# A hybrid DeltaNet and attention layer: diagonal blocks kept contiguous in DRAM and moved in few large DMAs, and the modulation's gate taken off TensorE

## The chip, the cores and the metric

The kernel runs on one core of a Trainium2 chip. The metric is the device time of one execution in microseconds (us). Three runs of the kernel before gave 2092.43, 2098.58 and 2100.68 us, so the median is 2098.58 us. The engines go by the profile's names: PE is TensorE (PEld its weight loads), DVE is VectorE, ACT is ScalarE, POOL is GpSimd and SP is SyncE, which issues most of the DMAs. An engine's name with a q (SPq) is its queue of DMA issues and waits.

## The reference

One layer of a diffusion backbone over 2048 latent tokens and 256 context tokens with a width of 1024, all in float32. What matters here, cut down:

```python
shift, scale, gate = jnp.split(jax.nn.silu(c) @ w_mod + b_mod, 3, axis=-1)
h = _rmsnorm(x, norm_w) * (1.0 + scale) + shift
# branch A: gated DeltaNet, 4 heads of 128, forwards and backwards, in chunks of 64:
a_mat = jnp.where(strict, jnp.einsum('nbhik,nbhjk->nbhij', kb, kc) * decay, 0.0)
t_mat = lax.linalg.triangular_solve(a_mat, eye, left_side=True, lower=True, unit_diagonal=True)
u = t_mat @ (vc * beta); w = t_mat @ (kb * exp(gc))         # and a scan over the chunks
# branch B: windowed attention with context keys and a sink; both branches gated:
y = sigmoid(ga) * (ya @ w_proj_a) + sigmoid(gb) * (yb @ w_proj_b)
x = x + gate[:, None] * (y @ w_out)
```

Two pieces of this are touched: the inverse of the unit lower triangular matrices of 64 by 64 (`t_mat`), one for each chunk of 64, head and direction, and the last third of the modulation, `gate`, a row of 1024 numbers that is needed only at the very end of the kernel.

## The kernel before

The kernel works through its stages in a fixed program: a Python function emits all instructions, and a scheduler with a timeline of its own sets the order on each engine when the program is built. Each engine then executes its list strictly in that order; SP's list holds the DMA issues. Matmuls of full accuracy are made of three (high part by high part, and two with a low part), so each weight tile is split into a high part on POOL (`wh`, L251) and a low part on DVE (`wl`, L252) after its DMA (`wr`, L250). A tile of weights for one group of 128 output channels is "a pair": two loads, two L251, two L252. Up to two pairs are held.

1. Up to about 118 us: modulation's shift and scale, the norms, and the normalised input `hh`, `hl`.
2. To about 630 us: the projections for q, k and v with short convolution (`qkv`, the tile `lps`), beside them the decays. For each key head and each 512 tokens `finish` multiplies keys by keys into `gps`, times the decays `dtl` (L607), and writes the result `p` and its transpose `pt` as full 128 by 128 blocks to DRAM (`Psp`, `PTsp`, L587): rows of 128 numbers, 512 bytes.
3. From about 620 to 963 us, the gates stage: `gates` (L814) runs 48 units of projections on PE (`rps`, L532 to L534, 24 matmuls a unit) for two of the four token groups. Beside them run two things. `mod_gate` computes the modulation's gate: it splits `w_mod` into high and low parts on POOL (`gwh` L227, `gwl` L228), multiplies them on PE (`gps` L230), adds two rows with a small matmul (`gsum` L236) and stores the row in `gsp`. And `base` inverts the triangular blocks on DVE: it fetches the two 64 by 64 diagonal blocks of each chunk of 128 and head, one block to a partition (`N`, L724, and the scale `nb`, L721), scales them (L725, L726), eliminates in 62 steps of two instructions (`btmp` L733, `N` L735), cuts the upper triangle off on POOL (L738), and writes the inverses to `Xsp` (L744). It does so twice, each time for 8 chunks and both directions; a third piece, `base4` (L748), does the last two chunks in another way.
4. From 963 to about 1385 us, the scan: 18 steps for both directions. `merge` builds the inverse for a chunk of 128 out of `Xsp` (`mx`, L966) and the off-diagonal block (`moff`, L968, read from `Psp` and `PTsp`); `chain` passes the state on; `output` writes results. More `rps` units fill the gaps on PE. Steps 1 to 8 need the first `base`, the next eight the second, the last two `base4`.
5. To the end: attention, projections of both branches, the output projection, where `gsp` is read.

The names in the program's order: `N`, `nb`, `btmp` are base's tiles; `x` (L1047, L1056), `S` (L1078) the scan's.

## Time and profile before

| what | value |
|---|---|
| runs | 2092.43, 2098.58, 2100.68 us; median 2098.58 us |
| the profiled execution's own time | 2097.5 us |
| its span, first to last instruction | 2095.8 us |
| PE busy | 1982.4 us, 95% |
| DVE, ACT, POOL busy | 1420.7, 751.5, 778.6 us |
| mean granted PE clock | 0.977 of full speed |
| DMA packets, bytes | 392748, 335.49 MB |

How to read the rows: a group's row names line, engine and operation, then what it writes and from what, the shape, the count, then its busy time and the mean of one instruction, and last how long the engine stood idle right before such instructions and what it waited for. A row of a table by stretches gives the stretch, its length, each engine's busy time with the number of instructions, the granted PE clock, the busy share of the DMA engines and GB/s. A row of the timeline gives start, duration and instruction, and in brackets the idle time before it. Matmuls are pipelined, so the modelled duration of one is longer than the distance between two starts, which is what counts.

### The profile page before, as it was taken

The numbers are of one execution on the slowest core, as the hardware profiler recorded it, in microseconds if no ns is written. First come the engines' busy times: TensorE is split into PE (matmuls) and PEld (weight loads), VectorE is DVE, ScalarE is ACT, GpSimd is POOL, SyncE is SP. The second block draws the span as 40 slices with busy tenths as digits, with TensorE's granted clock in tenths as the row PEclk, the third lists the DMA queues.
The fourth block names the chain that finished last, engine by engine and source line by source line (L and its number), as shares of the span: only waits on it lengthen the run. The fifth ranks groups of instructions, "written<-read, shape, count | busy, mean of one in ns | idle before, by whom it ended". The sixth has DMA issues, their size and how long they took to land.

```text
span 2095.8 us, 32306 instructions
## 1 busy us (share of the span) xinstructions
PE 1982.4 (95%) x11111; PEld 1650.2 (79%) x11111; DVE 1420.7 (68%) x2713; ACT 751.5 (36%) x1911; POOL 778.6 (37%) x920
## 2 busy tenths in 40 slices
PE   6999999999998789879988999999989999999999
PEld 3888888889986567667876888888878888878887
DVE  6888767767662799879945986644477777753322
ACT  5655555554441000001121223324466555541100
POOL 2862202255551356414232223422256454442321
PEclk8999999999999899999998999999999999999999
DMA  7452237754444533337567778855356555455542
GB/s 250 146 154 91 84 116 204 217 183 147 146 140 114 119 109 112 100 102 204 166 171 203 212 217 231 237 157 162 126 163 207 162 170 172 128 179 191 175 144 93
DMA packets 392748, 335.49 MB, mean 160 GB/s; under 512 B 83176, under 2 KB 318760, under 8 KB 392232
## 3 DMA queue, kind: packets, MB, share of 16 engines
q1 hardware_dynamic: 365160, 290.95, 48.0%
q10 hardware_dynamic: 27424, 42.48, 5.7%
q8 instruction: 88, 1.44, 0.3%
q14 instruction: 76, 0.62, 0.1%
HBM read 220.28 MB, written 111.49 MB: 158 GB/s over the span
## 4 chain that ended last, share of the span: by engine, by line
PE 67%; DVE 10%; DMA 9%; SPq 5%; POOL 4%; issue 3%; ACT 1%; POOLq 0%; DVEq 0%; ACTq 0%
PE rps L532 5%; PE rps L534 5%; PE rps L533 4%; PE lps L532 4%; PE lps L534 4%; PE lps L533 4%; PE ops L1270 3%; PE ops L1272 3%; PE ops L1271 3%; PE pt L920 3%; PE pps L1185 2%; PE pps L1187 2%; PE pps L1186 2%; DMA wr<-in_w_in_dram 2%; DVE btmp L733 2%
## 5 line engine op out<-in xcount | busy, mean ns | idle before, releaser
L532 PE MATMUL rps<-hh,wh 128*128 128x512 f32 x768 | 313.7, 408 | 6.9 <-DVE rt L798 5.6
L534 PE MATMUL rps<-hh,wl 128*128 128x512 f32 x768 | 312.1, 407 | 0.0
L533 PE MATMUL rps<-hl,wh 128*128 128x512 f32 x768 | 311.8, 406 | 0.0
L251 POOL TENSOR_SCALAR wh<-wr 128x512 fp32r<-128x512 f32 x120 | 105.5, 889 | 276.4 <-DMA wr<-in_w_in_dram 121.3
L796 ACT ACTIVATE rt<-rps 128x512 f32<-128x512 f32 x96 | 57.5, 599 | 387.5 <-PE rps L534 319.7
L532 PEld LDWEIGHTS rps<-hh,wh 128*128 128x128 f32 x768 | 147.9, 193 | 41.5 <-DVE rt L798 6.0
L534 PEld LDWEIGHTS rps<-hh,wl 128*128 128x128 f32 x768 | 147.9, 193 | 35.9 <-issue 2.2
L533 PEld LDWEIGHTS rps<-hl,wh 128*128 128x128 f32 x768 | 147.7, 192 | 32.5 <-issue 1.3
L532 PE MATMUL lps<-hh,wh 128*128 128x512 f32 (+1 forms) x448 | 171.9, 384 | 0.3 <-ACT y L632 0.3
L534 PE MATMUL lps<-hh,wl 128*128 128x512 f32 (+1 forms) x448 | 171.3, 382 | 0.0
L533 PE MATMUL lps<-hl,wh 128*128 128x512 f32 (+1 forms) x448 | 171.2, 382 | 0.0
L571 DVE SCALAR_TENSOR_TENSOR cacc<-y,cw,cacc 128x512 f32<-128x512 f32 (+1 forms) x224 | 160.4, 739 | 14.6 <-ACT cacc L569 11.8
L252 DVE TENSOR_TENSOR wl<-wr,wh 128x512 fp32r<-128x512 f32 x120 | 96.9, 818 | 66.6 <-POOL wh L251 64.4
L896 DVE CUSTOM_DVE_ANT_0 pr<-sc,band,sk 128x640 f32<-128x640 f32 (+1 forms) x128 | 106.7, 862 | 51.4 <-PE pt L920 25.9
L922 ACT CAST ph<-pt 128x512 fp32r<-128x512 f32 x156 | 90.4, 586 | 123.0 <-PE pt L920 92.5
L924 DVE TENSOR_TENSOR pl<-pt,ph 128x512 fp32r<-128x512 f32 x156 | 105.1, 685 | 37.1 <-ACT ph L922 36.4
L735 DVE TENSOR_TENSOR N<-N,btmp 128x62 f32<-128x62 f32 (+30 forms) x124 | 121.2, 978 | 2.7
L733 DVE TENSOR_TENSOR btmp<-N 128x62 f32<-128x62 f32 (+30 forms) x124 | 120.4, 971 | 3.0
L906 POOL TENSOR_SCALAR pr<-pr,sm 128x640 f32<-128x640 f32 (+1 forms) x128 | 99.8, 801 | 48.5 <-DVE sm L904 27.3
L898 ACT ACTIVATE pr<-pr,sm 128x640 f32<-128x640 f32 (+1 forms) x128 | 104.0, 815 | 20.2 <-DVE sm L896 19.9
L1185 PE MATMUL pps<-yh,wph 128*128 128x512 f32 x256 | 105.3, 415 | 3.9 <-ACT yh L1167 2.5
L1186 PE MATMUL pps<-yl,wph 128*128 128x512 f32 x256 | 101.6, 397 | 0.0
(307 smaller groups left out, 4974.6 us busy)
## 6 DMA issues: line engine op xcount, KB each, us to landing
wr<-in_w_in_dram SPq DMA_DIRECT2D x120, 256.0 KB
kw<-Ksp SPq DMA_DIRECT2D x28, 384.0 KB
x<-vsp SPq DMA_DIRECT2D x36, 256.0 KB
k<-ksp SPq DMA_DIRECT2D x34, 256.0 KB
kT<-kTsp SPq DMA_DIRECT2D x34, 256.0 KB
wm<-in_w_mod_dram SPq DMA_DIRECT2D x16, 512.0 KB
xt<-in_x_dram SPq DMA_DIRECT2D x16, 512.0 KB
dtl<-Dsp SPq DMA_DIRECT2D x32, 256.0 KB
```

The lines of the kernel that those rows point to most:

```text
L251: G.tensor_scalar(wh[:, k:k + 4], wr, 1.0, 1.0, op0=ALU.mult, op1=ALU.mult)
L532: T.matmul(ps, lhsT=wh[:, k], rhs=xh[:, k], start=k == 0, stop=False)
L533: T.matmul(ps, lhsT=wh[:, k], rhs=xl[:, k], start=False, stop=False)
L534: T.matmul(ps, lhsT=wl[:, k], rhs=xh[:, k], start=False, stop=k == kt - 1)
L571: V.scalar_tensor_tensor(a, y[:, t:t + n], cw[:, m, t:t + 1], a, op0=ALU.mult, op1=ALU.add)
L733: V.tensor_tensor(tv, A[:, m + 1:, m].unsqueeze(2).to_broadcast([h1 + n, r, m]), A[:, m, 0:m].unsqueeze(1).to_broadcast([h1 + n, r, m]), o ...
L735: V.tensor_tensor(A[:, m + 1:, 0:m], A[:, m + 1:, 0:m], tv, op=ALU.add)
L896: V.tensor_tensor_reduce(s_, ps[:, o:768], band[:, b0:b0 + W + 256], -0.125, sk[:, 1, hd:hd + 1], ALU.add, ALU.min, sm[:, h, 1:2])
L898: S.activation(s_, s_, AF.Exp, scale=-1.0, bias=sm[:, h, 1:2], accum_out=sm[:, h, 2:3])
L924: V.tensor_tensor(pl, pt, f32(ph), op=ALU.subtract)
L1185: T.matmul(ps, lhsT=wh[:, k, ms], rhs=hs[k], start=k == 0, stop=False)
L1186: T.matmul(ps, lhsT=wh[:, k, ms], rhs=ls[k], start=False, stop=False)
```

## The change

Three things are changed.

First, the DRAM layout. In place of `Psp` and `PTsp` there are `Nsp` (the two 64 by 64 diagonal blocks of a chunk and head, each contiguous) and `offsp` (the one off-diagonal block that `merge` reads), both for each direction. `finish` writes three pieces (`spill_blocks`) where it wrote one block. `base` then fetches runs of neighbouring chunks with one DMA each, and writes its inverses with one DMA for each direction to `Xset`; of each of these 8 chunks `merge` reads its part. `base4` fetches two chunks at once.

Second, in `base` the scaling on DVE and the select on POOL go over four pieces of 16 rows, and only over the columns that matter, where they went over the whole 64 by 64.

Third, `mod_gate` no longer uses PE for the product: ACT multiplies a tile of `w_mod` of 128 by 512 by the activated input (a number for each partition), POOL adds eight of these into `gacc`, and one matmul with a column of ones sums over the partitions; this happens twice, for 512 columns each.

```diff
@@ -94,11 +94,13 @@
     ksp = dscr("ksp", [NC, 128, H, 128])
     vsp = dscr("vsp", [NC, 128, H, 128])
     Dsp = dscr("Dsp", [NC, 128, H, 128])
-    Psp = dscr("Psp", [NC, 128, H, 128])
-    PTsp = dscr("PTsp", [NC, 128, H, 128])
+
+    Nsp = [dscr(f"Nsp{d}", [NC, H, 2, 64, 64]) for d in range(2)]
+    offsp = [dscr(f"offsp{d}", [NC, 64, H, 64]) for d in range(2)]
     QDsp = dscr("QDsp", [NB, 128, H, 128])
     brT = dscr("brT", [NC, 8, 128])
-    Xsp = [many(f"Xsp{d}_", NC, [H, 2, 64, 64]) for d in range(2)]
+    Xset = [many(f"Xsp{d}_", 2, [8, H, 2, 64, 64]) for d in range(2)]
+    Xsp = [{}, {}]
     X4sp = dscr("X4sp", [2, 2, 4, 8, 64, 16])
@@ -209,37 +211,26 @@
 
     def mod_gate(pool, ones):
 
-        for _ in range(3):
+
+        for n in range(2):
+            cs_ = slice(2 * D + n * 512, 2 * D + n * 512 + 512)
+            gacc = pool.tile([128, 512], F32, name="gacc", bufs=1)
+            for k in range(KT):
+                wm = pool.tile([128, 512], F32, name="wmg", bufs=2)
+                dma(wm, ins["w_mod"][0, k * 128:(k + 1) * 128, cs_])
+                S.activation(wm if k else gacc, wm, AF.Copy, scale=silc[:, k, 0:1])
+                if k:
+                    G.tensor_tensor(gacc, gacc, wm, op=ALU.add)
+                yield
             yield
-        sil2 = pool.tile([128, KT, 2], F32R, name="sil2", bufs=1)
-        V.tensor_copy(sil2[:, :, 0], silc[:, :, 0])
-        V.tensor_tensor(sil2[:, :, 1], silc[:, :, 0], f32(sil2[:, :, 0]), op=ALU.subtract)
-        for n in range(4):
-            gps = psum(f"gd{n % 2}", [2, 256], name=f"gps{n}")
-            ns = slice(n * 256, n * 256 + 256)
-            cs_ = slice(2 * D + n * 256, 2 * D + n * 256 + 256)
-            for k in range(0, KT, 2):
-                wm = wq.tile([128, 2, 256], F32, name="wmg", tag="wr")
-                dma(wm, ins["w_mod"][0, k * 128:(k + 2) * 128, cs_].rearrange("(k p) c -> p k c", p=128))
-                for j in range(2):
-                    wh = pool.tile([128, 256], F32R, name="gwh", bufs=1)
-                    wl = pool.tile([128, 256], F32R, name="gwl", bufs=1)
-                    G.tensor_scalar(wh, wm[:, j], 1.0, 1.0, op0=ALU.mult, op1=ALU.mult)
-                    G.tensor_tensor(wl, wm[:, j], f32(wh), op=ALU.subtract)
-                    for x in (wh, wl):
-                        T.matmul(gps, lhsT=sil2[:, k + j], rhs=x, start=k + j == 0 and x is wh,
-                                 stop=k + j == KT - 1 and x is wl)
-                yield
-            two = ev.tile([2, 256], F32, name="gtwo", tag="rt")
-            V.tensor_copy(two, gps)
-            gsum = psum(f"gd{n % 2}", [1, 256], name=f"gsum{n}")
-            T.matmul(gsum, lhsT=ones[0:2, 0:1], rhs=two, start=True, stop=True)
-            grow = ev.tile([1, 256], F32, name="grow", tag="rt")
+            gsum = psum(f"gd{n}", [1, 512], name=f"gsum{n}")
+            T.matmul(gsum, lhsT=ones[:, 0:1], rhs=gacc, start=True, stop=True)
+            grow = ev.tile([1, 512], F32, name="grow", tag="rt")
             dma(grow, ins["b_mod"][:, cs_])
             V.tensor_tensor(grow, gsum, grow, op=ALU.add)
             V.tensor_scalar(grow, grow, 0.5, None, op0=ALU.mult)
-            dma(gsp[:, ns], grow)
-        yield
+            dma(gsp[:, n * 512:n * 512 + 512], grow)
+            yield
 
@@ -578,6 +569,13 @@
         dma(dt, Dsp[c0:c0 + nn, :, h].rearrange("c p i -> p c i"))
         return dt
 
+    def spill_blocks(d, t, c0, nn, h):
+
+        for b in range(2):
+            r = slice(b * 64, b * 64 + 64)
+            dma(Nsp[d][c0:c0 + nn, h, b].rearrange("c r i -> r c i"), t[r, :, r])
+        dma(offsp[d][c0:c0 + nn, :, h].rearrange("c r i -> r c i"), t[64:128, :, 0:64])
+
...
@@ -605,7 +603,10 @@
                 T.matmul(gps[:, j], lhsT=zc[j] if m >= 4 else kT[:, j], rhs=zc[j], start=True, stop=True)
             p = pb.tile([128, 4, 128], F32, name="p", tag="o")[:, :nn]
             V.tensor_tensor(p, gps[:, :nn], dt, op=ALU.mult)
-            spill((Psp[c0:c0 + nn] if m >= 4 else QDsp[b0:b0 + nn])[:, :, h], p)
+            if m >= 4:
+                spill_blocks(1, p, c0, nn, h)
+            else:
+                spill(QDsp[b0:b0 + nn][:, :, h], p)
...
-            spill(PTsp[c0:c0 + nn, :, h], pt)
+            spill_blocks(0, pt, c0, nn, h)
 
@@ -705,7 +706,17 @@
     bs = bs_.__enter__()
 
 
-    def base(npool, pool, fr, bk):
+    def runs(chunks):
+
+        out = []
+        for i, c in enumerate(chunks):
+            if out and c == out[-1][1] + out[-1][2]:
+                out[-1][2] += 1
+            else:
+                out.append([i, c, 1])
+        return out
+
+    def base(si, npool, pool, fr, bk):
 
 
         n = 8 * len(fr)
@@ -716,14 +727,16 @@
             G.memset(N[0:h1], 0.0)
             G.memset(nb[0:h1], 0.0)
         for d, chunks in ((0, fr), (1, bk)):
-            for ci, c in enumerate(chunks):
-                p0 = d * h1 + ci * 8
-                dma(nb[p0:p0 + 8], brT[c, d * 4:d * 4 + 4].rearrange("h (b t) -> (h b) t", b=2))
-                for b in range(2):
-                    src = (PTsp, Psp)[d][c][b * 64:b * 64 + 64, :, b * 64:b * 64 + 64]
-                    dma(N[p0 + b:p0 + 8:2], src.rearrange("r h i -> h r i"))
-        V.tensor_tensor(N[0:h1], N[0:h1], nb[0:h1].unsqueeze(1).to_broadcast([h1, 64, 64]), op=ALU.mult)
-        V.tensor_tensor(N[h1:h1 + n], N[h1:h1 + n], nb[h1:h1 + n].unsqueeze(2).to_broadcast([n, 64, 64]), op=ALU.mult)
+            for i0, c, k in runs(chunks):
+                p0 = d * h1 + i0 * 8
+                dma(nb[p0:p0 + 8 * k], brT[c:c + k, d * 4:d * 4 + 4].rearrange("c h (b t) -> c (h b) t", b=2))
+                dma(N[p0:p0 + 8 * k], Nsp[d][c:c + k].rearrange("c h b r i -> (c h b) r i"))
+        for q in range(4):
+            r, w = slice(q * 16, q * 16 + 16), q * 16 + 16
+            V.tensor_tensor(N[0:h1, r, 0:w], N[0:h1, r, 0:w],
+                            nb[0:h1, 0:w].unsqueeze(1).to_broadcast([h1, 16, w]), op=ALU.mult)
+            V.tensor_tensor(N[h1:h1 + n, r, 0:w], N[h1:h1 + n, r, 0:w],
+                            nb[h1:h1 + n, r].unsqueeze(2).to_broadcast([n, 16, w]), op=ALU.mult)
         yield 9
         A = N[0:h1 + n]
         for m in range(1, 63):
@@ -735,13 +748,16 @@
-        G.affine_select(A, A, pattern=[[1, 64], [-1, 64]], base=0, channel_multiplier=0,
-                        compare_op=ALU.is_gt, fill=0.0)
+        for q in range(4):
+            r, w = slice(q * 16, q * 16 + 16), 64 - q * 16
+            G.affine_select(A[:, r, q * 16:], A[:, r, q * 16:], pattern=[[1, 16], [-1, w]], base=0,
+                            channel_multiplier=0, compare_op=ALU.is_gt, fill=0.0)
         V.memset(A.rearrange("p r c -> p (r c)")[:, ::65], 1.0)
         for d, chunks in ((0, fr), (1, bk)):
+            p0 = d * h1
+            dma(Xset[d][si].rearrange("c h b r j -> (c h b) (r j)"), N[p0:p0 + n].rearrange("p r j -> p (r j)"))
             for ci, c in enumerate(chunks):
-                p0 = d * h1 + ci * 8
-                dma(Xsp[d][c].rearrange("h b r c -> (h b) r c"), N[p0:p0 + 8])
+                Xsp[d][c] = Xset[d][si][ci]
         yield 1
 
     def base4(fr, bk):
@@ -755,12 +771,9 @@
         G.memset(nb[0:32], 1.0)
         G.memset(nc_, 1.0)
         for d, chunks in ((0, fr), (1, bk)):
-            for ci, c in enumerate(chunks):
-                p0 = d * 16 + ci * 8
-                dma((nc_, nb)[d][p0:p0 + 8], brT[c, d * 4:d * 4 + 4].rearrange("h (b t) -> (h b) t", b=2))
-                for b in range(2):
-                    src = (PTsp, Psp)[d][c][b * 64:b * 64 + 64, :, b * 64:b * 64 + 64]
-                    dma(N[p0 + b:p0 + 8:2], src.rearrange("r h i -> h r i"))
+            c, p0 = chunks[0], d * 16
+            dma((nc_, nb)[d][p0:p0 + 16], brT[c:c + 2, d * 4:d * 4 + 4].rearrange("c h (b t) -> c (h b) t", b=2))
+            dma(N[p0:p0 + 16], Nsp[d][c:c + 2].rearrange("c h b r i -> (c h b) r i"))
...
-    for fr, bk, np_ in (([0, 1] + LAT(*range(0, 6)), [0, 1] + LAT(*range(10, 16)), bs),
-                        (LAT(*range(6, 14)), LAT(*range(2, 10)), bs2)):
+    for si, (fr, bk, np_) in enumerate((([0, 1] + LAT(*range(0, 6)), [0, 1] + LAT(*range(10, 16)), bs),
+                                        (LAT(*range(6, 14)), LAT(*range(2, 10)), bs2))):
-            for _ in base(np_, bs2, fr, bk):
+            for _ in base(si, np_, bs2, fr, bk):
...
                 dma(X[b * 64:b * 64 + 64, :, b * 64:b * 64 + 64], Xsp[d][c][:, b].rearrange("h r c -> r h c"))
         off = pool.tile([128, H, 64], F32, name=f"moff{d}", bufs=2)
-        dma(off[64:128], (PTsp, Psp)[d][c][64:128, :, 0:64])
+        dma(off[64:128], offsp[d][c])
```

The order on the engines, from the built programs. PE in the gates stage; `rps` are the gates' own matmuls, `gps` the modulation's. Before, from the eighth unit of the stage on, it reads:

```order
L534 MATMUL rps<-hh_441,wl 128x512
L532 MATMUL rps<-hh_441,wh 128x512
L533 MATMUL rps<-hl_442,wh 128x512
L230 MATMUL gps_7833<-gwh,sil_7830 2x256
L534 MATMUL rps<-hh_441,wl 128x512
L532 MATMUL rps<-hh_441,wh 128x512
L230 MATMUL gps_7833<-gwl,sil_7830 2x256
L533 MATMUL rps<-hl_442,wh 128x512
```

and so on, 64 `gps` and 4 `gsum` in all (the trace counts each `gsum` twice, for two passes). After it, the only matmuls of the modulation in this stage are two `gsum`, the first of which stands 19 units into the stage:

```order
L523 MATMUL rps<-hh_155,wh 128x512
L524 MATMUL rps<-hl_156,wh 128x512
L525 MATMUL rps<-hh_155,wl 128x512
L227 MATMUL gsum_8317<-gacc,mats 1x512
L523 MATMUL rps<-hh_411,wh 128x512
L524 MATMUL rps<-hl_412,wh 128x512
```

In both programs the first matmul of the scan stands behind the same number of units, 49.7 counted from the stage's first.

SP's list at the start of the stage, where `base` is fed. Before:

```order
L721 DMA nb<-brT 8x64
L724 DMA N<-PTsp 4x64x64
L799 DMA zasp_149<-rt 128x512
L724 DMA N<-PTsp 4x64x64
L587 DMA QDsp<-p 128x4x128
L721 DMA nb<-brT 8x64
L724 DMA N<-PTsp 4x64x64 x2
L721 DMA nb<-brT 8x64
```

After:

```order
L732 DMA nb<-brT 64x1x64
L733 DMA N<-Nsp_89 64x4096
L812 DMA zasp_119<-rt 128x512
L585 DMA QDsp<-p 128x4x128
L732 DMA nb<-brT 16x1x64
L733 DMA N<-Nsp_90 16x4096
L732 DMA nb<-brT 48x1x64
L733 DMA N<-Nsp_90 48x4096
L241 DMA wr<-in_w_in_dram 128x4x128
```

For the two calls of `base`, 96 issues (32 `nb`, 64 `N`) became 10 (5 and 5).

DVE at the same place; L252 and L243 are the same line of `weights`, L798 and L811 the same of `rest_run`. Before:

```order
L252 TENSOR_TENSOR wl<-wr,wh 128x512
L725 TENSOR_TENSOR N<-N,nb 64x4096
L798 SCALAR_TENSOR_TENSOR rt<-rt,rps 128x512
L252 TENSOR_TENSOR wl<-wr,wh 128x512
L798 SCALAR_TENSOR_TENSOR rt<-rt,rps 128x512
L252 TENSOR_TENSOR wl<-wr,wh 128x512
L798 SCALAR_TENSOR_TENSOR rt<-rt,rps 128x512
L252 TENSOR_TENSOR wl<-wr,wh 128x512
L726 TENSOR_TENSOR N<-N,nb 64x4096
```

After:

```order
L736 TENSOR_TENSOR N<-N,nb 64x16x16
L736 TENSOR_TENSOR N<-N,nb 64x16x32
L736 TENSOR_TENSOR N<-N,nb 64x16x48
L736 TENSOR_TENSOR N<-N,nb 64x1024
L243 TENSOR_TENSOR wl<-wr,wh 128x512
L811 SCALAR_TENSOR_TENSOR rt<-rt,rps 128x512
L243 TENSOR_TENSOR wl<-wr,wh 128x512
L738 TENSOR_TENSOR N<-N,nb 64x16x16
L738 TENSOR_TENSOR N<-N,nb 64x16x32
L738 TENSOR_TENSOR N<-N,nb 64x16x48
L738 TENSOR_TENSOR N<-N,nb 64x1024
```

The scaling stands about two pairs of weights earlier, and the first elimination follows three pairs earlier. From there the steps lie closer: ahead of the scan's first L1056 stand 233 of the 248 elimination instructions, where 212 stood before. POOL's list has 14 additions to `gacc` in place of 64 instructions for `gwh` and `gwl`, and its eight selects stand between the `wh` of the pairs, each behind the elimination step that it waits for.

## The prediction

> **What bounds the kernel now.** I read the page first, then the busy times by stretches, then PE's and DVE's groups in the stretch that stood out.
>
> ```profile
> span 2095.8 us, 32306 instructions
> PE 1982.4 (95%) x11111; PEld 1650.2 (79%) x11111; DVE 1420.7 (68%) x2713; ACT 751.5 (36%) x1911; POOL 778.6 (37%) x920
> ```
>
> PE bounds the whole: 2095.8 - 1982.4 = 113 us are idle. The question is where they lie. Busy times by stretches (the first is the gates stage, the second the scan's start, the last the key projections):
>
> ```profile
> core 0: us, PE busy (x) PEld busy (x) DVE busy (x) ACT busy (x) POOL busy (x), PEclk, DMA share, GB/s
> 640.00:963.00 323.00, 278.94 (x1170) 211.53 (x1169) 250.44 (x273) 27.57 (x46) 118.58 (x117) 0.95 0.41 109
> 963.00:1100.00 137.00, 128.93 (x876) 110.02 (x875) 104.67 (x190) 26.51 (x70) 43.62 (x53) 0.94 0.69 188
> ...
> 310.00:424.00 114.00, 112.36 (x692) 97.99 (x691) 83.37 (x162) 67.03 (x222) 29.49 (x30) 1.00 0.74 211
> ```
>
> The gates stage alone has 323 - 278.94 = 44 us of PE's idle time. PE's groups in it:
>
> ```profile
> L533 PE MATMUL rps<-hl,wh 128*128 128x512 f32 x366 | 148.5, 406 | 0.0
> L532 PE MATMUL rps<-hh,wh 128*128 128x512 f32 x366 | 148.3, 405 | 5.6 <-DVE rt L798 5.6
> ...
> L230 PE MATMUL gps<-gwh,sil 128*2 128x256 f32 x32 | 9.2, 289 | 23.1 <-POOL gwh L227 23.1
> L230 PE MATMUL gps<-gwl,sil 128*2 128x256 f32 x32 | 9.2, 288 | 5.7 <-POOL gwl L228 5.6
> L236 PE MATMUL gsum<-gtwo,mats 2*1 2x256 f32 x8 | 2.8, 430 | 9.7 <-DVE gtwo L234 9.7
> ```
>
> Nearly all of it stands before the modulation's own matmuls: 23.1 + 5.7 + 9.7 = 38.5 us; the other 5.6 us is a wait for `rt` on DVE. PE never waits for a weight pair here. What a matmul really costs, from the timeline:
>
> ```profile
> 656.03 0.39 PE L534 MATMUL rps<-hh,wl 128*128 128x512 f32 x1
> ...
> 657.43 0.40 PE L534 MATMUL rps<-hh,wl 128*128 128x512 f32 x1
> ...
> 663.38 0.79 PE L532 MATMUL rps<-hh,wh 128*128 128x512 f32 x1 [5.56 <-DVE rt L798]
> ...
> 668.67 0.47 PE L532 MATMUL rps<-hh,wh 128*128 128x512 f32 x1
> ...
> 670.80 0.28 PE L230 MATMUL gps<-gwl,sil 128*2 128x256 f32 x1
> 670.92 0.40 PE L533 MATMUL rps<-hl,wh 128*128 128x512 f32 x1
> ...
> 907.09 1.01 PE L236 MATMUL gsum<-gtwo,mats 2*1 2x256 f32 x2 [9.71 <-DVE gtwo L234]
> ```
>
> Six matmuls lie between the first two rows: 1.40 / 6 = 0.233 us each. Twelve lie between the next two: 5.29 / 12 = 0.44 us, so a wait of 5.6 us is followed by matmuls at about half rate, and costs 12 x 0.21 = 2.5 us more. A `gps` takes 670.92 - 670.80 = 0.12 us.
>
> **The gates stage without its waits.** It holds 3 x 366 = 1098 `rps`: 1098 x 0.233 = 256 us of the 323. The rest, 67 us, is made of 44.1 us of waits, 64 x 0.12 = 7.7 us of `gps`, 4 x 1.0 = 4 us of `gsum`, and by difference 11 us of half-rate matmuls, about four waits' worth at 2.5 us. The order rows show that after the change no `gps` is left and the scan begins behind the same 49.7 units. So 38.5 + 7.7 + 11 us go. Of `gsum` I keep 2 us: two matmuls of twice the columns, instead of four. That the two don't wait: in POOL's order the last addition into each `gacc` stands some five weight pairs, or ten units of 24 x 0.233 = 5.6 us, ahead of the first `gsum` and eight pairs ahead of the second.
>
> The 5.6 us wait for `rt`, and base's start (DVE's groups in the stage, two rows of SP's issues with their durations and first and last start, a row of the timeline, one of the chain of waits):
>
> ```profile
> L725 DVE TENSOR_TENSOR N<-N,nb 64x4096 f32<-64x4096 f32 x2 | 8.8, 4417 | 18.8 <-DMA nb<-brT 18.8
> L726 DVE TENSOR_TENSOR N<-N,nb 64x4096 f32<-64x4096 f32 x2 | 8.8, 4422 | 11.4 <-DMA nb<-brT 9.1 <-issue 2.3
> L721 SPq DMA_DIRECT2D nb<-brT x32: 310/1086/2167, 624.0 to 728.7; - x32
> L724 SPq DMA_DIRECT2D N<-PTsp x32: 593/627/1376, 624.6 to 704.9; - x32
> ...
> 688.99 0.75 DVE L733 TENSOR_TENSOR btmp<-N 128x62 f32<-128x62 f32 x1
> 1140.14 9.34 DMA N<-N
> ```
>
> SP issued base's loads from 624.0 to 728.7 us; DVE stood 18.8 + 11.4 us for them, `rt` queued behind. Now there are ten issues. How long a load of 64 rows of 16 KB takes isn't shown; the nearest row is the copy of `N` (three of 512 KB in 9.34 us, 6.2 us a megabyte), and below it stands nothing but the DMA share in this stretch, 0.41, which says there is room. I take 6 us a megabyte: the first load lands near 632, the second near 638 us, and the first elimination can start near 644 instead of 688.99 us. The 5.6 us go, and I put back 3 us since DVE meets these waits earlier in its list, with `rt` and a weight pair behind them. Sum for the stage: -5.6 - 38.5 - 7.7 - 2 - 11 + 3 = **-62 us**.
>
> **DVE must keep up.** PE's stage shrinks to some 260 us, and the same eliminations have to fit beside it (groups in the stage of DVE and POOL, then of the whole span the nearest rows for an addition on POOL and a scaled copy on ACT, and the scan's first `ksps` in the chain of waits):
>
> ```profile
> L735 DVE TENSOR_TENSOR N<-N,btmp 128x62 f32<-128x62 f32 (+30 forms) x97 | 97.0, 1000 | 2.4
> L733 DVE TENSOR_TENSOR btmp<-N 128x62 f32<-128x62 f32 (+30 forms) x97 | 94.4, 973 | 2.5
> L252 DVE TENSOR_TENSOR wl<-wr,wh 128x512 fp32r<-128x512 f32 x46 | 35.1, 773 | 36.6 <-POOL wh L251 36.6
> L228 POOL TENSOR_TENSOR gwl<-wmg,gwh 128x256 fp32r<-128x256 f32 x32 | 37.8, 1182 | 2.5 <-PE gps L230 0.2
> L227 POOL TENSOR_SCALAR gwh<-wmg 128x256 fp32r<-128x256 f32 x32 | 23.6, 738 | 52.0 <-DMA wmg<-in_w_mod_dram 45.9 <-PE rps L532 3.4 <-PE gps L230 1.0
> L1153 POOL TENSOR_TENSOR wpl<-wpr,wph 128x512 fp32r<-128x512 f32 x16 | 20.4, 1296 | 10.7 <-ACT wph L1152 10.7
> L569 ACT ACTIVATE cacc<-y,cw 128x512 f32<-128x512 f32 (+1 forms) x56 | 38.3, 693 | 2.5 <-DMA cw<-in_conv_w_dram 1.3 <-DVE g L186 0.8
> 997.90 1.53 PE ksps L1054 x12
> ```
>
> Between base's start and the scan's first L1056 stand 233 elimination instructions at (97.0 + 94.4) / 194 = 0.99 us, 230 us; 25 weight pairs at 2 x 0.77, 39 us; and some 25 us of `rt`, the second base's scaling and the scan's first work. That is 294 us from 644, so 938 us. PE reaches the scan at 640 + 256 + 2 + 3 = 901 us, and from there the first `ksps` was 997.90 - 963 = 35 us away: 936 us. The two meet within 2 us, so DVE is no longer cover but a second bound. Against a delay: POOL's 37.8 + 23.6 = 61.4 us for the gate become 14 additions of 128 by 512, at 1.3 us (nearest row, L1153) 18 us, and the scaling shrinks by piece to 2560 of 4096 columns, 4 x (4.42 - 2.76) = 6.6 us in all, already counted. For a delay: nothing evens out inside single pairs. I charge **+5 us**; the ends are 0 and, if the eliminations run a tenth slower, +29. ACT's 16 products at 0.69 us (L569, also a scaled copy) are 11 us on an engine busy 27.57 of 323, behind which the `tanh` waits; I cost them at nothing, and return to it below. The select, split likewise, comes off POOL's list piece by piece and hides behind the `wh`, which wait for loads anyway.
>
> **The scan.** Two of PE's waits hang on what the change moves:
>
> ```profile
> PE mtp L974 <- POOL x L1047: 6.5, 1, 6.5
> PE mtp L974 <- DMA mx<-Xsp: 6.2, 1, 6.2
> L744 SPq DMA_DIRECT2D Xsp<-N x32: 285/651/2372, 872.8 to 1096.3; - x32
> ```
>
> The second base's 16 writes reach to 1096.3 us, in one list with the scan's own loads, up to 2.4 us an issue. They become two, and in DVE's new order base ends behind the first step that has an `x`, where it ended behind the third. Step 9 then finds its inverses, and the loads of `x` aren't queued behind writes. Both waits and their half-rate time go: -12.7 - 2 x 2.5 = **-18 us**. The bound on the other side is 0, if the scan waits elsewhere.
>
> **The key projections pay.**
>
> ```profile
> DVE p L607 <- DMA dtl<-Dsp: 6.2, 5, 2.1
> L587 SPq DMA_DIRECT2D Psp<-p x20: 359/360/611, 301.9 to 423.6; - x20
> ```
>
> Each of 40 writes becomes three: 80 more issues at 0.36 us, 29 us more on SP in about 114, with `dtl` and the weights behind them, some 1 us later each time. Rows: 36 full-size writes (16 full and 4 half, twice) of 512 rows of 512 bytes become 768 rows of 256. In this stretch the DMA engines were busy 0.74 x 16 x 114 = 1350 us for 24.1 MB, 47 thousand rows of 512 bytes, 29 ns each. If a half row costs half, DMA time falls, and PE, busy 112.36 of 114, gains nothing. If it costs the same, 9200 more rows add 265 us, and the share goes to 0.89. The trace shows no DRAM write of 256-byte rows; I take the same price, since the reads of 256-byte rows for `N` left the share at 0.41 beside the weights. PE then waits for `p` a little more often than the 6.2 us that DVE waits now: **+6 us**, between 0 and the rival below.
>
> [...]
>
> **Sum.** -62 + 5 - 18 + 6 = -69 us on the profiled run's 2097.5 us: 2028.5. That run lies 1.1 us under the median, so it makes no difference; I round to **2030 us**. Later stages have the same instructions; I expect nothing from them.
>
> **Rivals.**
> A. *DVE takes over.* The eliminations run at 0.99 us or worse and PE waits for weight pairs. For it: DVE is busy 250.44 of 323 now. Against: POOL disturbs less. Its upper price, 29 us in place of 5: about 2053. Chance 0.17.
> B. *The gate's new chain is the new wait.* ACT executes in order, its `tanh` frees PE's accumulators, and a product waits for a 256 KB load just when base's megabytes are fetched. For it: POOL waited 45.9 us for these loads. Against: two units of slack, and the first `gsum` ten units behind. Were half of the 38.5 us lost again: about 2050. Chance 0.10.
> C. *Half rows cost double* (57 ns). The writes take 27.6 thousand x 57 ns = 1580 us instead of 530: the share becomes 1.31, the stretch 36 us longer, 30 above my charge: 2060. Chance 0.10.
> D. *The weights bound the stage.* POOL's `wh` is ready late anyway, and PE's waits move to the pairs. Against: PE waits for no pair in the groups above. Half of the 62 us stays: about 2060. Chance 0.05.
> E. *Slower.* The same place as C, at a price that eats all: 69 us + 6 in a stretch of 114 means a share of 1.66, 3030 us of DMA, 80 ns a row. From 80 ns, 2.8 times the measured row, the kernel is slower; at 100 ns the stretch grows by another 34 us, 2130. Chance 0.04.
>
> **How the numbers follow.** The forecast has 0.54: between 2005 (no DVE charge, no charge in the projections, and a third wait of the scan gone) and 2045. The range reaches over A to D to **2005 to 2068**. About 0.5% (10 us) can be told from no change. Only E is slower; a mixture of C, A and D near zero has 0.03. Faster 0.93, same 0.03, slower 0.04.
>
> **What would show it.** Right: PE's groups in the gates stage without idle time, the scan's first matmul near 900 us, the first elimination near 645, DVE close to full until some 940, no wait for `mx`. Wrong: PE waiting for `wl` (A) or `rt` behind ACT (B); DMA share near 1 and waits for `dtl` between 310 and 430 us (C, E).

## The result, and the profile after

The change takes **2047.58 us** (median of four runs, 2046.15 to 2049.45) where the kernel before takes 2097.22 (2092.43 to 2100.68): a ratio of 0.9763, with a 95% interval from 0.9748 to 0.9778. The prediction was 2030 us, between 2005 and 2068. The gain is 50 us and not 68, and the time lies 2.6 us above the narrower interval, 2005 to 2045, to which the forecast itself gave a chance of 0.54.

The page of the profiled run, and its busy times by the stretches that the prediction used:

```profile
span 2044.3 us, 32068 instructions
PE 1966.8 (96%) x11043; PEld 1643.2 (80%) x11043; DVE 1421.5 (70%) x2715; ACT 760.4 (37%) x1927; POOL 742.9 (36%) x876
```

```profile
core 0: us, PE busy (x) PEld busy (x) DVE busy (x) ACT busy (x) POOL busy (x), PEclk, DMA share, GB/s
640.00:963.00 323.00, 312.39 (x1377) 247.20 (x1375) 302.15 (x342) 46.89 (x84) 111.32 (x94) 0.98 0.51 143
...
310.00:424.00 114.00, 108.47 (x645) 92.36 (x643) 74.68 (x144) 60.33 (x198) 24.86 (x27) 1.00 0.68 172
```

PE's idle time in the first stretch fell from 44 to 10.6 us, with DVE busy 302 of 323 us there. In the last stretch, the key projections, PE did less: 108.47 us busy where it was 112.36, with a *lower* DMA share (0.68, before 0.74).

The stretches are at fixed times, while the stages moved. So the rest of this text uses stages, cut at four instructions: the first gates matmul (`rps`), the scan's first matmul (`mtp`), the scan's last `fps`, and the end. The scan's columns are read together with the last one, since gates units left over fill the scan or follow it. All values are starts in the profiled runs, or differences of them:

| kernel | median us | first `rps` | first elimination | gates stage | scan | scan's end to end | first `rps` to end |
|---|---|---|---|---|---|---|---|
| before | 2097.2 | 615.1 | 689.0 | 349.0 | 449.8 | 681.9 | 1480.7 |
| the change | 2047.6 | 631.8 | 662.9 | 297.3 | 429.6 | 685.6 | 1412.5 |
| gate_alone | 2091.8 | 617.1 | 706.8 | 331.2 | 464.4 | 683.2 | 1478.8 |
| blocks_alone | 2062.3 | 630.5 | 662.3 | 316.2 | 415.7 | 696.6 | 1428.5 |
| whole | 2051.2 | 632.3 | 664.1 | 292.2 | 437.2 | 685.0 | 1414.4 |
| many_loads | 2075.4 | 631.8 | 698.7 | 313.6 | 446.7 | 683.0 | 1443.3 |
| dtl_act | 2033.6 | 619.0 | 649.4 | 292.8 | 434.3 | 686.4 | 1413.5 |
| merged | 2039.5 | 622.3 | 659.3 | 294.1 | 429.5 | 690.4 | 1414.0 |
| merged_dtl_act | 2023.8 | 612.8 | 648.7 | 294.0 | 441.9 | 672.6 | 1408.5 |

From the first two rows: the projections lose 16.7 us, the gates stage gains 51.7, the scan 20.2, and 3.7 are lost after it. The sum is -51.5 us between the two spans.

PE's groups in the gates stage of the change (columns: busy, mean ns of one, idle time before them):

```profile
L523 PE MATMUL rps<-hh,wh 128*128 128x512 f32 x398 | 158.7, 399 | 6.5 <-DVE rt L811 4.7 <-POOL wh L242 1.7
L525 PE MATMUL rps<-hh,wl 128*128 128x512 f32 x397 | 159.5, 402 | 1.6 <-DVE wl L243 1.6
L227 PE MATMUL gsum<-gacc,mats 128*1 128x512 f32 x4 | 2.0, 590 | 0.0
```

The new `gsum` matmuls don't wait at all. The 8.1 us of idle time that are left stand before `rt`, `wh` and `wl`, which DVE and POOL make.

DVE's groups of the scaling in the same stage, and the row of base's eliminations (duration of one: least, median, most; first and last start):

```profile
L738 DVE TENSOR_TENSOR N<-N,nb 64x256 f32<-64x256 f32 (+3 forms) x8 | 7.7, 1009 | 7.0 <-DMA N<-Nsp 7.0
L736 DVE TENSOR_TENSOR N<-N,nb 64x256 f32<-64x256 f32 (+3 forms) x8 | 6.0, 812 | 5.2 <-DMA N<-Nsp 5.2
```

```profile
L746 DVE TENSOR_TENSOR btmp<-N x124: 218/1036/2136, 662.9 to 977.8; 128x62 f32<-128x62 f32 x4, 128x122 f32<-128x122 f32 x4, 128x180 f32<-128x180 f32 x4, 128x236 f32<-128x236 f32 x4
```

DVE's waits for base's data fell from 30 to 12 us, and the scaling from 17.6 to 13.7 us of work, 3.9 us less where the prediction had 6.6.

### The profile page after: what moved, and what is told of

Same layout as the page of the kernel before. It is cut to its first block, busy times and chain, and to the rows that moved or that the text cites. A ratio compares the mean times of both kernels' runs of the same rounds, so it can differ in the third digit from the quotient of the medians.

```text
span 2044.3 us, 32068 instructions
## 1 busy us (share of the span) xinstructions
PE 1966.8 (96%) x11043; PEld 1643.2 (80%) x11043; DVE 1421.5 (70%) x2715; ACT 760.4 (37%) x1927; POOL 742.9 (36%) x876
## 5 line engine op out<-in xcount | busy, mean ns | idle before, releaser
L909 DVE CUSTOM_DVE_ANT_0 pr<-sc,band,sk 128x640 f32<-128x640 f32 (+1 forms) x128 | 106.4, 863 | 42.5 <-PE sc L905 22.1
L243 DVE TENSOR_TENSOR wl<-wr,wh 128x512 fp32r<-128x512 f32 x120 | 94.0, 796 | 18.1 <-POOL wh L242 17.9
```

The costliest lines, as they stand in the source:

```text
L909: V.tensor_tensor_reduce(s_, ps[:, o:768], band[:, b0:b0 + W + 256], -0.125, sk[:, 1, hd:hd + 1], ALU.add, ALU.min, sm[:, h, 1:2])
```

## Which part brings the gain

Two kernels take the change apart. **gate_alone** is the kernel before with the new gate:

```diff
 def mod_gate(pool, ones):
-    ...   # 64 gps matmuls on wh/wl pairs, 4 gsum
+    ...   # 16 products on ACT, 14 additions on POOL, 2 gsum
```

> The kernel before with the new gate alone (products on ACT, additions on POOL, two gsum matmuls); block layout, loads and scaling as before. By the prediction's own sum: of the gates stage's -62 us the gate's share is 38.5 + 7.7 + most of the 11 + 2, less the 3 put back, some -55 us where DVE does not object. But the elimination still starts near 689 us, 44 us later than in the change, and DVE's 294 us from there end near 983 us, with the scan's first matmul about 35 us ahead of that: near 945 instead of 964 us. So if DVE is a second bound, the gate alone brings only some -20 us here (2077). If DVE is no bound, -55 us (2042). The scan keeps its two waits for x.

Measured: 2091.75 us, ratio 0.9973 (0.9955 to 0.999): 6 us faster, between 2 and 9 by the interval. PE's waits in its gates stage:

```profile
PE rps L521 <- DVE rt L787: 25.7, 3, 9.3
PE rps L523 <- DVE wl L241: 9.8, 3, 6.1
PE rps L521 <- POOL wh L240: 0.6, 1, 0.6
```

The 38.5 us before `gps` and `gsum` are gone, and 36.1 us of other waits stand in their place. They wait for DVE, which waits for base's loads: its four scalings of base start at 668.0, 700.5, 727.7 and 754.2 us, after waits of 9.9, 12.6, 9.4 and 8.8 us, and PE's four longest waits of the stage end 6 to 7 us after each of them. One such pair (the wait of the scaling is for several DMAs, and the profile names the one that landed last):

```profile
700.53 4.42 DVE L715 TENSOR_TENSOR N<-N,nb 64x4096 f32<-64x4096 f32 x1 [12.62 <-DMA zbsp<-rt]
```

```profile
706.42 0.77 PE L521 MATMUL rps<-hh,wh 128*128 128x512 f32 x1 [7.29 <-DVE rt L787]
```

The first elimination comes at 706.8 us, even later than the 689.0 of before. The scan does begin at 948.3 us, 16 us earlier and about where expected, but its end hardly moves (1412.7 us, before 1413.9). It meets inverses that aren't there yet, in PE's waits from 948 to 1420 us:

```profile
PE mtp L963 <- DMA mx<-Xsp: 12.0, 4, 10.0
PE myp L980 <- DVE my L978: 8.7, 2, 5.7
PE ops L1095 <- DVE oa L1092: 6.0, 2, 3.7
```

So the expectation was right that DVE objects, and even too kind. Rival B's chain shows, too: ACT waits 48.4 us for `w_mod` loads in this stage, and DVE 26.8 us for ACT's `rt`. In the change ACT waits as long (48.7 us), but DVE only 0.3 us for `rt`.

**blocks_alone** is the change with the old gate:

```diff
 def mod_gate(pool, ones):
-    ...   # 16 products on ACT, 14 additions on POOL, 2 gsum
+    ...   # 64 gps matmuls on wh/wl pairs, 4 gsum
```

> The change without its gate: blocks contiguous, few large DMAs, scaling and select in pieces, and the modulation's gate on PE as before. By the prediction's terms: -5.6 us (rt) - 18 us (scan) in favour. By the comparison of the two traces the key projections lose 14 to 20 us instead of the 6 forecast. So -24 + 6 = -18 us (2079) by the prediction, and -24 + 17 = -7 us (2090) by what the trace of the change shows. First elimination near 645 us, as in the change.

Measured: 2062.33 us, ratio 0.9835 (0.9799 to 0.9871), some 17 to 28 us better than expected. PE's waits in its gates stage:

```profile
PE gps L232 <- POOL gwh L229: 11.4, 6, 4.4
PE gps L232 <- POOL gwl L230: 2.8, 5, 0.8
PE rps L534 <- DVE rt L822: 2.2, 2, 1.9
```

The waits of `gps` fell from 28.7 to 14.2 us and the one of `gsum`, 9.7 us, vanished, with the gate's code as it was. So these waits stood at the gate, but went with what changed around `base`. The trace of before shows two places. At 688.6 us `gps` had waited 6.5 us, right behind a scaling of base for which DVE had waited 9.1. And 17.5 us of the 38.5 stand between 881 and 907 us, behind base's first writes: SP waited 13.0 us for DVE to finish the inverses, and then issued 16 writes with the loads of weights and `w_mod` between them. SP's list of before from 872 to 898 us, and the two writes that blocks_alone has in their place:

```profile
872.77 0.64 SPq L744 DMA_DIRECT2D Xsp<-N  x2
...
877.31 8.12 SPq L744 DMA_DIRECT2D Xsp<-N  x6
...
886.40 11.24 SPq L744 DMA_DIRECT2D Xsp<-N  x8
```

```profile
827.88 1.14 SPq L769 DMA_DIRECT2D Xsp<-N  x2
```

No run separates the writes from the loads. In blocks_alone the eliminations end at 982 us instead of 1052, and the scan at 1362 instead of 1414.

From the first `rps` to the end the four kernels give 1480.7, 1478.8 (gate), 1428.5 (blocks) and 1412.5 us (both): the gate is worth 2 us by itself and 16 beside the blocks, the blocks 52 by themselves and 66 beside the gate. The profiled run of gate_alone took 2097.88 us, 6 us more than the median, so its 1478.8 may be some 6 us too long. By the medians of the whole times the gate is worth 6 us by itself and 15 beside the blocks, the blocks 36 by themselves and 44 beside the gate, with their loss in the projections included. The gains hang together either way, but less by the medians.

**many_loads** is the change with base's loads issued by single chunks (32 of `N`, 32 of `nb`, instead of 5 each):

```diff
-            if out and c == out[-1][1] + out[-1][2]:
+            if False:
```

> The change, with base's loads issued chunk by chunk, 64 KB of contiguous DRAM each (32 loads of N and 32 of nb for the two batches, instead of 5 and 5); contiguous layout, pieces and gate as in the change. It tells which part of the base's 30 us of waits in the kernel before was SP's number of issues and which the scattered reads. If the issues (0.5 to 0.7 us each on SP, 54 more): the first elimination comes some 10 us later for the first batch (673 instead of 663), and the weights and modulation loads behind it late too: 2053 to 2060. If the scattered reads were the cost, nothing changes: 2047.

Measured: 2075.38 us, ratio 0.9895 (0.9859 to 0.9932), 28 us above the change and more than expected. One row of SP's issues, SP's three longest waits between 640 and 722 us, and PE's waits in the gates stage:

```profile
L732 SPq DMA_DIRECT2D nb<-brT x32: 263/292/743, 640.5 to 721.5; - x32
```

```profile
SPq L732 <- DMA N<-Nsp: 7.7, 9, 2.1
SPq L812 <- DVE rt L811: 6.8, 4, 2.6
SPq L220 <- POOL gacc L223: 4.9, 3, 2.2
```

```profile
PE rps L523 <- DVE rt L811: 12.9, 4, 5.4
PE rps L523 <- POOL wh L242: 4.2, 1, 4.2
PE rps L525 <- DVE wl L243: 3.3, 2, 2.9
```

An issue is short, 0.29 us, so 54 of them are 16 us. Yet they spread over 81 us, because in SP's one list they stand between spills (L812), which wait for their data, and modulation loads (L220), which wait for their buffer, and because SP, before an issue, often waits for an earlier load of base to land (L732). The first elimination comes 36 us later (698.7), and PE waits for `rt` again. So the number of loads alone, with contiguous reads, accounts for 28 of the 44 us that the blocks bring beside the gate by the medians (31 of 66 from the first `rps` to the end). What the scattered reads were worth was not measured by itself; in the kernel before the issues of `nb` took 1.09 us (median) beside them.

**whole** is the change without its pieces:

```diff
-        for q in range(4):
-            ...   # scaling of 16 rows and their 16, 32, 48, 64 columns
+        V.tensor_tensor(N[0:h1], N[0:h1], nb[0:h1]...)       # all 64 rows and columns
+        V.tensor_tensor(N[h1:h1 + n], N[h1:h1 + n], nb[h1:h1 + n]...)
...
-        for q in range(4):
-            ...   # select of 16 rows
+        G.affine_select(A, A, ...)
```

> The change without its pieces: base scales the two halves of the batch with one instruction each (4.4 us) over all 4096 columns, and selects with one POOL instruction, as before; everything else as in the change. By the prediction's terms the pieces are worth 4 x (4.42 - 2.76) = 6.6 us of DVE, on an engine that is the second bound, and POOL's list is not held by one long select: between 0 and 7 us slower than the change, taken 4: 2052. If the eliminations do not set PE's end any more, 0: 2047.5.

Measured: 2051.17 us, ratio 0.9783 (0.9747 to 0.982). That is 3.6 us above the change, as expected, but the two intervals overlap: a gain of the pieces isn't shown.

## What the key projections pay for

The largest miss of the prediction is here: 16.7 us instead of 6. `dtl`, the decay block, has one buffer. Its next load can go out only when DVE has made `p`; in SP's list the writes of `p` stand between the two, and sometimes others, and the traces show that list executed in its order (in the kernel before, the nine issues from base's first `nb` on start between 623.98 and 629.41 us, as the program lists them). One such step, SP's list of before (the row of `p` is DVE's):

```profile
351.45 0.69 DVE L607 TENSOR_TENSOR p<-gps,dtl 128x512 f32<-128x512 f32 x1 [0.93 <-PE gps L605]
352.17 0.36 SPq L587 DMA_DIRECT2D Psp<-p  x1
352.62 0.46 SPq L578 DMA_DIRECT2D dtl<-Dsp  x1
```

And of the change:

```profile
365.31 0.69 DVE L605 TENSOR_TENSOR p<-gps,dtl 128x512 f32<-128x512 f32 x1 [2.25 <-DMA dtl<-Dsp]
366.03 1.23 SPq L576 DMA_DIRECT2D Nsp<-p  x2
367.31 0.61 SPq L577 DMA_DIRECT2D offsp<-p  x1
368.02 0.55 SPq L585 DMA_DIRECT2D ksp<-st  x1
368.62 0.53 SPq L569 DMA_DIRECT2D dtl<-Dsp  x1
```

From the end of `p` to the end of the next `dtl` issue it is 0.94 us before and 3.15 after; over all blocks between 296 and 446 us the mean is **1.2 us before (21 blocks) and 3.9 after (19)**. Of these 3.9 us the three writes of `p` are 2.0 (the one write of before 0.4), and writes of `pt`, `ksp` and `kTsp`, which the new order has ahead of `dtl` more often, are 0.9 (before 0.1). The new writes also take longer to issue, 0.60 us against 0.36:

```profile
L576 SPq DMA_DIRECT2D Nsp<-p x40: 574/597/2035, 301.1 to 441.6; - x40
```

DVE's waits for `dtl` between 290 and 470 us, of before and of the change:

```profile
DVE p L607 <- DMA dtl<-Dsp: 8.2, 6, 2.1
```

```profile
DVE p L605 <- DMA dtl<-Dsp: 22.1, 14, 3.0
```

Two theories were on trial: the issues on SP, or the price of 256-byte rows on the DMA engines (rival C). **pt_on_act** gave the first form of the former a try: SP has too many issues, so half of the new writes go to ACT's queue.

```diff
...          # spill_blocks takes the queue as an argument
-            spill_blocks(0, pt, c0, nn, h)
+            spill_blocks(0, pt, c0, nn, h, adma)
```

> The change, with the three writes of each transposed block (pt) issued from ACT's queue instead of SP's: same bytes, same rows of 256 bytes, 60 issues fewer on SP between 300 and 447 us, 60 more on ACT. Theory 1 (SP's list of issues is the bound: 0.6 us a write, so that dtl and the next reuse of pt come late): the waits for dtl fall from 26 us to near the 11 us of the kernel before, PE's idle time between 340 and 460 us falls from 13 us to about 5, and the time by about 8 us, to 2039. Theory 2 (rows of 256 bytes cost DMA time, whoever issues them): no change, 2047. Against both: ACT is busy 85 of 145 us there and 60 issues of 0.6 us are 36 us more on its list; if ACT becomes the bound the time rises above 2050.

Measured: 2047.27 us, ratio 0.9761 (0.9731 to 0.9791): no change, and the theories are not told apart by that. DVE's waits for `dtl` did fall, from 22.1 to 14.0 us, yet the first `rps` came at 631.7 us, as in the change. In this form the first theory falls, as its SP list shows, with two rows of DVE behind it:

```profile
418.94 1.69 SPq L569 DMA_DIRECT2D dtl<-Dsp  x1
424.22 1.24 SPq L576 DMA_DIRECT2D Nsp<-p  x2
425.50 0.61 SPq L577 DMA_DIRECT2D offsp<-p  x1
426.21 0.55 SPq L585 DMA_DIRECT2D ksp<-st  x1
426.86 0.48 SPq L591 DMA_DIRECT2D kTsp<-cacc  x1
427.39 0.55 SPq L569 DMA_DIRECT2D dtl<-Dsp  x1
```

```profile
423.50 0.69 DVE L605 TENSOR_TENSOR p<-gps,dtl 128x512 f32<-128x512 f32 x1 [3.64 <-DMA dtl<-Dsp]
431.73 0.69 DVE L605 TENSOR_TENSOR p<-gps,dtl 128x512 f32<-128x512 f32 x1 [3.92 <-DMA offsp<-pt]
```

SP issues nothing for 3.6 us ahead of the second row, so its list as a whole isn't full. What counts is the part between `p` and `dtl`, and most of that is the writes of `p`, which this kernel left on SP (the mean lag fell only from 3.9 to 3.4 us). Besides, `p` now waited for a buffer that a late write of `pt` from ACT still held.

**rows256** and **three_issues** separate the two theories on the kernel before: one writes rows of 256 bytes with one DMA a block, the other rows of 512 bytes with three.

```diff
# rows256: two halves of 64 columns, one DMA
-    Psp = dscr("Psp", [NC, 128, H, 128])
-    PTsp = dscr("PTsp", [NC, 128, H, 128])
+    Psp = dscr("Psp", [NC, 2, 128, H, 64])
+    PTsp = dscr("PTsp", [NC, 2, 128, H, 64])
...          # the writes and all reads follow this layout
# three_issues: the layout as before, three DMAs of 64, 32 and 32 partitions
-            spill(PTsp[c0:c0 + nn, :, h], pt)
+            for r in (slice(0, 64), slice(64, 96), slice(96, 128)):
+                dma(PTsp[c0:c0 + nn, r, h].rearrange("c p d -> p c d"), pt[r])
```

> The kernel before; only the DRAM arrays of the decayed products and their transposes are laid out in two halves of 64 columns, so that each write puts 256-byte rows where it put 512-byte rows, still with one DMA a block on SP (40 writes, 1024 rows each instead of 512). Nothing else changes (base and the scan read the same 256-byte pieces). Theory 2 (the price of small rows on the DMA engines delays the key projections): the DMA share between 310 and 424 us rises above 0.74, the first gates matmul comes some 10 us or more after 615 us, the time is about 2108. Theory 1 (the number of issues on SP does it): no change, 615 us and 2098. A third way: the issue itself gets longer with the number of rows (0.36 us now); then SP's list is longer by 40 times that.

> The kernel before; only each write of a block (128 partitions, rows of 512 bytes) is issued as three DMAs by partitions (64, 32 and 32), with the same rows and bytes. 80 more issues on SP, as in the change. Theory 1 (SP's issues): the first gates matmul comes late by about as much as in the change without its gate, 15 us, so near 630 us, and the time is about 2108, if the rest follows. Theory 2 (row price): no change, 615 us and 2098.

Measured: rows256 takes 2098.73 us, ratio 1.0004 (0.999 to 1.0018), with its first `rps` at 614.0 us. Its stretch of the projections and its writes:

```profile
310.00:424.00 114.00, 112.52 (x697) 98.28 (x695) 84.97 (x162) 66.50 (x223) 30.58 (x30) 1.00 0.82 212
```

```profile
L588 SPq DMA_DIRECT2D Psp<-p x20: 359/370/963, 301.3 to 422.9; - x20
```

The DMA share rose from 0.74 to 0.82, and DVE's waits for `dtl` stayed (8.0 us, before 8.2). three_issues takes 2107.78 us, ratio 1.0057 (1.0042 to 1.0072), first `rps` at 623.3; its writes and DVE's waits for `dtl`:

```profile
L588 SPq DMA_DIRECT2D Psp<-p x60: 426/581/1936, 299.2 to 433.1; - x60
```

```profile
DVE p L609 <- DMA dtl<-Dsp: 19.0, 13, 2.8
```

The rows cost no time here; the issues do. But 8.2 us of delay are half of the change's 16.7. **three_256** does both at once (rows256 with its write in three pieces, as above):

> The kernel before, with three issues a block on SP and rows of 256 bytes at once. Three issues alone brought the first gates matmul from 615.1 to 623.3 us and rows alone to 614.0, the change itself to 631.8 (630.5 without its gate). If small rows cost only where the writes already land late (the next p or pt waits for its buffer), the two together reach 630 us and 2115. If the rows are free in every case, 623 us and 2108 as with three issues alone, and the other 8 us of the change come from something else (the order of the work, or the shape of its writes).

Measured: 2112.24 us, ratio 1.0066 (1.0046 to 1.0086), first `rps` at 623.9 us. By that the rows are free beside the issues, too, but the profiled run took 2103.97 us, 8 us less than the median. By the medians three_256 is 4.5 us slower than three_issues, with intervals that overlap, so a small price of the rows beside the issues is neither shown nor excluded.

Where the other half of the change's delay comes from is not settled. Little of it is in DVE's waits for `dtl`, 22.1 us in the change and 19.0 in three_issues, and between 310 and 424 us PE loses about as much in both (busy 108.5 and 109.0 us). The difference opens between 420 and 460 us, where PE is busy 32.0 us in the change and 36.8 in three_issues. There PE waits for `qh`, which DVE makes for the attention; these waits between 290 and 630 us, of the change and of three_issues:

```profile
PE zt L475 <- DVE qh L472: 6.2, 3, 3.7
```

```profile
PE zt L484 <- DVE qh L481: 1.4, 3, 0.6
```

What makes `qh` late was not tested.

**dtl_act** is the change with the `dtl` loads on ACT's queue, and **before_dtl_act** the same edit on the kernel before:

```diff
-        dma(dt, Dsp[c0:c0 + nn, :, h].rearrange("c p i -> p c i"))
+        adma(dt, Dsp[c0:c0 + nn, :, h].rearrange("c p i -> p c i"))
```

> The change, with only the decay loads (dtl, 36 issues) moved from SP's queue to ACT's. dtl has one buffer, so its next load can be issued only when DVE has made p, and in SP's list it stands behind the three writes of p (1.9 us) and whatever waits ahead of them. Theory 1, in the form that the runs so far leave (the writes stand ahead of dtl on SP): waits for dtl between 290 and 470 us fall from 22 us to below 10, the first gates matmul comes near 622 us instead of 632, the time is near 2038. If the three writes hurt in another way (the buffers of p and pt come free late): waits for dtl fall, but the first gates matmul stays near 630 and the time at 2046. If ACT, in order, gets stuck behind p: later than 632 us, above 2050.

> The kernel before, with only the decay loads (dtl) moved from SP's queue to ACT's: the control for dtl_act. If the 13 us that dtl_act gained over the change were the change's own loss given back, the kernel before, whose DVE waits only 8 us for dtl, gains at most 2 to 3 us: first gates matmul near 613, time near 2095. If moving dtl is a gain of its own whatever the writes, the first gates matmul comes near 606 and the time is near 2089.

Measured: dtl_act takes 2033.63 us, ratio 0.9706 (0.9691 to 0.972), first `rps` at 619.0, the mean lag 0.5 us, and of DVE's waits for `dtl` between 290 and 470 us this is left:

```profile
DVE p L605 <- DMA dtl<-Dsp: 0.6, 1, 0.6
```

before_dtl_act takes 2096.51 us, ratio 1.0003 (0.9984 to 1.0022), first `rps` at 615.3. So the edit is worth 14 us where three writes stand ahead of `dtl` and nothing where one does: what dtl_act gains is the change's own loss given back. Against its control it still pays 3.7 us in the projections.

**merged** writes two pieces a block instead of three (the lower 64 rows whole), for which base loads each run with two DMAs; **merged_dtl_act** has this and the edit of dtl_act:

```diff
-        for b in range(2):
-            r = slice(b * 64, b * 64 + 64)
-            dma(Nsp[d][c0:c0 + nn, h, b].rearrange("c r i -> r c i"), t[r, :, r])
-        dma(offsp[d][c0:c0 + nn, :, h].rearrange("c r i -> r c i"), t[64:128, :, 0:64])
+        dma(Nup[d][c0:c0 + nn, h].rearrange("c r i -> r c i"), t[0:64, :, 0:64])
+        dma(Nlo[d][c0:c0 + nn, h].rearrange("c r i -> r c i"), t[64:128])
...          # base loads each run with two DMAs, and the scan reads from Nlo
```

> The change with two writes a block instead of three: the lower 64 rows go whole (rows of 512 bytes, off-diagonal and diagonal block together) into one array, the upper diagonal block into another; base then loads each half of its batch with two DMAs (the lower blocks as 256-byte pieces), and the scan reads its off-diagonal blocks from the joint array. 40 issues fewer on SP, 256 KB a block more or less unchanged, a third fewer DRAM rows in the writes. Theory 1 (SP's issues at 0.6 us): 40 x 0.6 = 24 us of SP's list less in 145 us, the projections get back about two thirds of what they lost beyond the kernel before: some -6 us, 2041. Theory 2 (price of 256-byte rows): rows of the writes fall from 768 to 512 a block; a similar gain, with a DMA share that falls too. The two are told apart by pt_on_act; here the question is whether fewer issues are worth the harder loads of base (later first elimination, after 645 us).

> The change with both: two writes a block instead of three, and the decay loads on ACT's queue. If the two causes are one and the same list, the gains do not add: the first gates matmul near 617 us (622 with the merged writes alone), the time near 2034. If dtl on ACT is worth nothing beside the merged writes: 2039.5.

Measured: merged 2039.54 us, ratio 0.9727 (0.9696 to 0.9757), first `rps` at 622.3, lag 2.8 us. merged_dtl_act takes **2023.76 us**, ratio 0.9662 (0.9645 to 0.9678), 24 us below the change and 73 below the kernel before; its first `rps` at 612.8 us is ahead of even the kernel before. It gained 10 us more than expected. The projections gave 9.5 us by the first edit, 12.8 by the second and 19.0 by both, so the gains add for the most part. With `dtl` off SP, fewer writes still help; the likely reason, that `p` and `pt` get their buffers back sooner, was not tested alone.

## Why the prediction was right, and where it was wrong

The time lies in the range, 18 us above the point and 2.6 us outside the interval of the forecast: the range reaches it by the room left for the rivals, though none of them happened as written. By the steps of the sum:

- **"The key projections pay", +6: wrong in size, and the largest miss.** Measured +16.7. The mechanism was named (80 more issues on SP with `dtl` behind them), but the step "80 more issues at 0.36 us" took the price of a 128-partition write for writes of 64 partitions, which took 0.60 us; and "some 1 us later each time" was 2.7 us (1.2 to 3.9). That makes the issues dearer, but explains only half of the 16.7 us, as three_issues shows. The step also asked about DMA time, of which there was plenty (a share of 0.68 between 310 and 424 us).
- **Gates stage, -62 and DVE +5: close, for a wrong reason.** Measured -51.7 against -57. The prediction put 38.5 us of waits and most of the 7.7, 2 and 11 us down to the gate's matmuls. Alone, the new gate gives 6 us. The waits stood at `gps`, but they moved to `rt`, `wl` and the scan's `mx` as long as base was late. The blocks, which the prediction credited with 5.6 us in this stage (base's loads), bring most of the gain. That the sum came out near is in part luck: gate and blocks were changed at once, so what was credited to the wrong one doesn't show in the total.
- **"DVE is no longer cover but a second bound": right.** DVE is busy 302 of 323 us, and in gate_alone, where base starts late, its lateness takes most of the gain away. If the whole miss of the stage is put down to DVE, the charge of 5 us was some 5 too small; no run shows that it is.
- **First elimination near 645 us: 662.9.** Base's first issue comes 16.5 us later (640.5 instead of 624.0), behind the late projections. In relation to that, the estimate of the loads was right within some 2 us (22.4 us from there to the first elimination, 20 expected).
- **Scan, -18: right.** Measured -20.2, with neither wait, for `x` or for `mx`, in the change. 3.7 us of it return behind the scan.
- **Later stages, 0: right** but for those 3.7 us.

Of the rivals, A (DVE takes over) comes nearest in gate_alone, but there DVE stood still for base's loads and did not eliminate too slowly; in the change it costs the 8.1 us of waits at most. B did not happen: `gsum` waits 0.0 us. D did not either: PE's waits for `wh` and `wl` in the stage are 3.3 us. C and E fall with rows256: in that kernel some 17 thousand rows more (36 writes of 512 more, times 114/124 of the time) cost 0.08 x 16 x 114 = 146 us of DMA time, so by this estimate two half rows cost 8.6 ns more than a whole one of 29, or 19 ns each. A byte in half rows costs more DMA time here, about 1.3 times by the estimate. The doubled price of a row, rival C's 57 ns, was a supposition that no run shows, and the time didn't change (a ratio of 1.0004). The sign that the prediction gave for C and E, waits for `dtl` together with a DMA share near 1, came only by its first half. It had no rival for waits for `dtl` with a *falling* share, which is what SP's issue list, executed in its order, showed here.

## What to carry to other kernels

A wait belongs to the engine whose lateness causes it, not to the instruction that shows it: before crediting an edit with a row of idle time, ask what is late behind the releaser, since a wait that only one of two late things is cured of can move elsewhere (in gate_alone 38.5 us at the gate became 36.1 us of other waits). When a DMA is split, count what stands between a buffer's release and the issue of its next load on the same in-order queue, price each issue by a row of its own shape and place in the list (0.60 us here, where a write of another shape took 0.36), and, if it grows, put that load on another queue (14 us here). Merging many small loads paid here by where they stand in the queue, among issues that wait, more than by their own durations: 54 issues of 0.29 us are 16 us, and many_loads lost 28.

## What the runs showed of the hardware

In these runs the duration of an issue on SP did not follow its bytes or rows. A write of 128 partitions took 0.36 us with 512-byte rows and 0.37 with twice as many 256-byte rows; writes of 64 or 32 partitions with fewer rows took 0.58 (three_issues) and 0.60 us (the change, 64 partitions). The duration differed with what was issued just before, too. `ksp<-st`, 128 partitions, took 0.36 us at 357.06 us of before, with nothing issued right ahead of it, and 0.55 right behind `offsp` in the rows of the change above. Loads of eight partitions of `nb` took 1.09 us in the kernel before, where they stand among loads of 256 short rows, and 0.29 in many_loads, among loads of eight long ones.

Nor did it follow the DMA engines' busy share: between 310 and 424 us that fell from 0.74 before to 0.68 in the change, while the writes' issues grew from 0.36 to 0.60 us. Why the writes of fewer partitions took longer is open.
